# A two-block fp32 network on one core: index scores in tiles of their own, three gates behind the attention's output projection, and input rows scaled on TensorE

## The chip, the core and the metric

The kernel runs as one program on one core of one Trainium2 chip. The metric is the device time of one execution in microseconds (us); the time before is 1074.39 us, the median of three runs. A core has TensorE (PE, matmuls), VectorE (DVE), ScalarE (ACT), GpSimd (POOL) and SyncE (SP, which issues the large transfers).

## What is computed

Two blocks over 256 rows of 1024 channels, in fp32. The first has a conv branch and a sparse-attention branch that share one input projection, gates on both, and a feed-forward part; the second block (two mixers with feed-forward parts) is not touched by the change. Cut to the part that is touched:

```python
stream = concat([meta, x])                      # 16 meta rows + 256 rows, 1024 channels
h = rms_norm(stream, mix_norm_g)
u_conv, q, k, v, q_idx, k_idx, w_idx, gates = split(h @ w_in)
q, k, q_idx, k_idx = rope(...)                  # rotary embedding
a, gate = split(u_conv)                         # conv branch
c = causal_depthwise_conv(a * sigmoid(gate), conv_dw_w, conv_dw_b)      # 31 taps
y_a = silu(layer_norm(c, conv_ln_g, conv_ln_b)) @ conv_pw_out
dots = einsum("qhd,sd->qhs", q_idx, k_idx) * 64 ** -0.5                 # 8 index heads
score = einsum("qh,qhs->qs", w_idx * 8 ** -0.5, relu(dots))
idx = top_k(score with the meta rows always in)                         # a mask for each query
y_b = softmax(q @ k.T over the chosen keys) @ v @ w_o                   # 8 heads of 128
g_a, g_b = split(sigmoid(gates))
stream = stream + (g_a * y_a + g_b * y_b) @ w_merge_out
```

## The kernel before

Channels lie on partitions: the normed input is hT, eight tiles of 128 channels by 272 rows (or 258 rows, the last two meta rows and the 256 others, where only these are wanted). Each fp32 operand of a large product is split into a high part and the rest (whi and wlo of a weight, hT_h and hT_l of an input), and a product is three matmuls, whi with hT_h, whi with hT_l and wlo with hT_h (lines 175 to 177). So a projection to 128 output channels (`proj_tile`) is 24 matmuls into one PSUM buffer of four (ps_acc), and takes one half of a weight chunk. A chunk comes by one transfer on SP (wraw, three buffers); for each half, 128 x 1024, ACT copies the high part (whi, line 134) and DVE subtracts it (wlo, line 136), into six buffers that PE frees by reading them (`emit_split`, `next_half`). Smaller products, transposes and scores go through four other PSUM buffers (ps_wk).

The order of the work on an engine is set when the program is built: a scheduler places the instructions by their dependencies and priorities, parts under a high priority go first, and in the first stretch the order of PE, DVE and ACT is that of the code. At run time each engine takes its instructions in that order, and stands where one waits.

The stretch that the change touches runs from 0 to about 222 us:

- *Start* (lines 282 to 367). A warm-up of WARM = 9 fp32 matmuls of ones (L283); transposes of the 16 meta rows mt (L299); `turn` (L294) transposes the two 128-row tiles of x, eight 128 x 128 blocks each, into px, four PSUM buffers. ACT and DVE sum the squares of the rows (L305, L306, L307, L312), POOL takes the root (L233, a power of -0.5), and `spread` (L290) transposes the roots of all rows, repeated, so that they lie as a row over all partitions (rw). `scaled` (L329, DVE) multiplies px by that row into h, ACT makes hT_h of it with the norm's gain (L333), DVE hT_l (L344). The first two conv projections are interleaved by the list FIRST (L358), the other 14 follow (`proj_tile`).
- *Conv* (lines 365 to 423). 31 taps on 8 tiles: most on DVE (L389), some as products on ACT (L406), which are added by DVE (L412) or, into ysum, by transfers on POOL's queue that add in memory (L410); two rows L423 at the end add ysum.
- *Index scores* (`index_scores`, a generator that its callers advance): for each of two row tiles t and each of 8 heads a matmul (L474) into a ps_wk buffer, a Relu on ACT (L477) into r, one of two buffers of the tag s1, and a weighted sum on DVE (L478).
- *k, v, q projections*, then 16 gate projections in pairs (j = 0 for the conv branch's, j = 1 for the attention's; tanh on ACT into tg, L611), and between them the attention heads in steps: `attend_first` (the two meta rows as queries: L578, L580, L595) is advanced between the first gates, then `attend` of each head i behind gate pair i: scores (L553), softmax (`soft`, L534 and L538 on DVE, L537 and L539 on ACT), transposes (L556, L558), and after every fourth head the product with v (L566, L568).
- *End of the stretch.* The attention's output projection takes oT (8 projections of 24 matmuls; DVE adds the gate, L664). Under high priority the layer norm (LN) of the conv result yc: sums over tiles on DVE (L645, L646), over channels on PE (L648), yc minus the mean (L650), squares on ACT (L652), their sum on DVE (L654), over channels on PE (`rstd_row`, L631, L633 on DVE, the root L635 on POOL, its spread L638 on PE), then yc by the root (L658), Silu (L659) and the split into sT_h and sT_l (L200, L202). The conv's projections read sT (8 of 24 matmuls), and everything behind follows from both. POOL also clears a tile for the second reading of the meta rows (MEMSET mt_again, L677).

Of the kernel before, what the change touches and what calls it, by code (L numbers as in the profile page):

```python
# [59 lines left out]
WARM = 9  # L60
FIRST = []
for _k in range(KT + 1):
    for _j in range(2):
        FIRST += [(_j, 0, 0, _k)] if _k < KT else []
        FIRST += [(_j, 0, 1, _k - 1)] if _k else []
    FIRST += [(0, 1, 0, 3 * (_k - 5) + _i) for _i in range(3) if _k > 4 and 3 * (_k - 5) + _i < KT]
FIRST += [(1, 1, 0, _k) for _k in range(KT)]
PACE = 2
LATER = mybir.DependencyInfo(mybir.DependencyClass.NoSync, mybir.DependencyReason.DATA)
# [15 lines left out]
def tile_hybrid(ctx: ExitStack, tc: tile.TileContext, x, meta, wts, misc, vec, cst, rows, gkw, ng, pos,  # L85
# [36 lines left out]
    def emit_split(upto, later=None):  # L122
        while state["split"] < min(upto, 2 * N_CHUNKS):
# [10 lines left out]
            A.activation(hi, r, AF.Copy)  # L134
# [53 lines left out]
    def proj_tile(ps, xT, a, b, late=False):  # L188
        w = next_half()
        if late:  # L190
# [90 lines left out]
    pj = ps_acc()  # L281
    for _ in range(WARM):
        PE.matmul(pj[:, :P], ones, ones, start=True, stop=True)  # L283
    px = [ps_wk() for _ in range(4)]
    pm = pj[:, :P]
    pr = pj[:, P:P + L]
    rw = mp.tile([P, L], F32, name="rw", tag="sco", bufs=2)
    hm = sc.tile([P, KT, META], F32, name="hm", tag="s3", bufs=3)
    def spread(r, a, n):
        PE.transpose(pr[:, a:a + n], r.to_broadcast([n, P]), ident[:n, :n])  # L290

    def turn(t):
        for k in range(KT):
            PE.transpose(px[k // 2][:, (k % 2) * SEQ + t * P:(k % 2) * SEQ + (t + 1) * P],  # L294
                         xt[t][:, k * P:(k + 1) * P], ident)

    with tc.high_priority(), tc.manual_schedule(engines={ENG.PE, ENG.DVE, ENG.Activation}):
        for k in range(KT):
            PE.transpose(pm[:, k * META:(k + 1) * META], mt[:, k * P:(k + 1) * P], ident[:META, :META])  # L299
        turn(0)  # L300
        sm_ = sc.tile([P, 4], F32, name="sm_", tag="st", bufs=6)
        rm = sc.tile([P, 4], F32, name="rm", tag="st", bufs=6)
        ss = sc.tile([P, 4], F32, name="ss", tag="st", bufs=6)
        rs = sc.tile([P, 4], F32, name="rs", tag="st", bufs=6)
        A.activation(xn[2][:META], mt, AF.Square, accum_out=sm_[:META, 0:1])  # L305
        A.activation(xn[0], xt[0], AF.Square, accum_out=ss[:, 0:1])  # L306
# [9 lines left out]
        for t in range(2):  # L316
            spread(rs[:, t:t + 1], META + t * P, P)
# [18 lines left out]
        for q in range(4):  # L336
            high(2 * q)
            high(2 * q + 1)
            if q == 0:
                emit_split(2, later)  # L340
# [266 lines left out]
    for i in range(KT):  # L607
# [7 lines left out]
        for a in live:  # L615
            next(a)
# [702 lines left out]
```

## Time and profile before

| | |
|---|---|
| three runs | 1075.55, 1074.39, 1074.29 us; median 1074.39 us |
| the profiled execution | 1076.28 us; its span, first to last instruction, 1074.5 us |
| PE busy | 1054.8 us, 98% of the span |
| DVE busy | 739.5 us, 69% |
| ACT busy | 601.0 us, 56% |
| POOL busy | 44.1 us, 4% |
| transfers | 192.37 MB, mean 179 GB/s |

The profiled execution is one of its own and 1.89 us longer than the median; 1.78 us of it lie outside the span. Times of rows are from the start of the span. Matmuls are pipelined, so their durations overlap, and what one costs is the distance from start to start. An engine's idle time is put down to the instruction that released the waiting one. A share of the whole span is a mean over stretches with different limits.

### The profile page before, as it was taken

The page shows a single profiled execution, that of the slowest core. Times are in us where ns is not written, and L with a number is a line of the kernel's source. Part 1 is how long each engine was busy: PE and PEld are TensorE (multiplying, and loading weights), DVE is VectorE, ACT ScalarE, POOL GpSimd, SP SyncE. Part 2 cuts the span into 40 slices and gives each one's busy share as a digit, 9 for nine tenths or more (in the row PEclk, how much of TensorE's full clock was granted, in tenths as well). Part 3 has the DMA queues.
Part 4 walks back from the last instruction along what each step waited for, and adds up shares of the span by engine and source line. Part 5 has one row for each costly group of instructions (what it writes and reads, how often), then busy time and mean ns, then how long its engine had stood idle before and what let it go on. Part 6 is the DMA issues. An engine that isn't in the chain of part 4 may idle for free. (4 is left out here: it accounts for less than half of the span.)

```text
span 1074.5 us, 17515 instructions
## 1 busy us (share of the span) xinstructions
PE 1054.8 (98%) x6989; PEld 954.5 (89%) x6989; DVE 739.5 (69%) x1291; ACT 601.0 (56%) x1051; POOL 44.1 (4%) x52
## 2 busy tenths in 40 slices
PE   8999999999999999999999999999999999999997
PEld 8998998899899999977877999999888878999995
DVE  6899999995776767774577655556674766555555
ACT  6897698564555555567463444446256925444440
POOL 0131002100000000000000000000000000000000
PEclk8999999999999999999999999999999999999999
DMA  8886556564354555454453655557263436555541
GB/s 307 246 201 161 191 166 178 148 220 169 142 197 160 195 182 192 174 185 139 153 202 112 236 196 179 180 191 274 79 215 138 164 131 226 187 195 194 173 144 40
DMA packets 33333, 192.37 MB, mean 179 GB/s; under 512 B 3889, under 2 KB 7857, under 8 KB 12002
## 3 DMA queue, kind: packets, MB, share of 16 engines
q1 hardware_dynamic: 28002, 185.02, 49.7%
q0 software_dynamic: 5248, 6.23, 3.6%
q8 instruction: 55, 0.90, 0.3%
q14 instruction: 28, 0.23, 0.1%
HBM read 183.96 MB, written 1.05 MB: 172 GB/s over the span
## 5 line engine op out<-in xcount | busy, mean ns | idle before, releaser
L136 DVE TENSOR_TENSOR wlo<-wraw,whi 128x1024 fp32r<-128x1024 f32 x320 | 388.5, 1223 | 204.8 <-ACT whi L134 203.9
L134 ACT ACTIVATE whi<-wraw 128x1024 fp32r<-128x1024 f32 x322 | 337.3, 1058 | 302.0 <-PE ps_wk L176 117.7
L176 PE MATMUL ps_wk<-hT_l,whi 128*128 128x256 f32 (+1 forms) x976 | 274.9, 282 | 0.0
L177 PE MATMUL ps_wk<-hT_h,wlo 128*128 128x256 f32 (+1 forms) x976 | 274.6, 281 | 0.0
L175 PE MATMUL ps_wk<-hT_h,whi 128*128 128x256 f32 (+1 forms) x976 | 274.2, 281 | 0.0
L175 PEld LDWEIGHTS ps_wk<-hT_h,whi 128*128 128x128 f32 x976 | 184.4, 189 | 1.1
L176 PEld LDWEIGHTS ps_wk<-hT_l,whi 128*128 128x128 f32 x976 | 184.0, 189 | 1.4
L177 PEld LDWEIGHTS ps_wk<-hT_h,wlo 128*128 128x128 f32 x976 | 184.8, 189 | 0.4
L181 PE MATMUL ps_acc<-whi,rg_h 128*128 128x512 f32 x328 | 131.1, 400 | 0.0
L182 PE MATMUL ps_acc<-wlo,rg_h 128*128 128x512 f32 x328 | 129.6, 395 | 0.0
L183 PE MATMUL ps_acc<-whi,rg_l 128*128 128x512 f32 x328 | 127.1, 395 | 0.0
L175 PE MATMUL ps_acc<-hT_h,whi 128*128 128x258 f32 (+2 forms) x352 | 101.9, 290 | 0.0
L177 PE MATMUL ps_acc<-hT_h,wlo 128*128 128x258 f32 (+2 forms) x352 | 100.7, 286 | 0.0
L176 PE MATMUL ps_acc<-hT_l,whi 128*128 128x258 f32 (+2 forms) x352 | 100.5, 285 | 0.0
L183 PEld LDWEIGHTS ps_acc<-whi,rg_l 128*128 128x128 f32 x328 | 61.6, 188 | 14.7 <-DVE rg_l L202 0.2
L181 PEld LDWEIGHTS ps_acc<-whi,rg_h 128*128 128x128 f32 x328 | 61.6, 188 | 14.1 <-ACT rg_h L200 0.2
L182 PEld LDWEIGHTS ps_acc<-wlo,rg_h 128*128 128x128 f32 x328 | 61.7, 188 | 12.8
L181 PE MATMUL ps_acc<-whi,hT_h 128*128 128x512 f32 (+1 forms) x184 | 71.8, 390 | 0.0
L183 PE MATMUL ps_acc<-whi,hT_l 128*128 128x512 f32 (+1 forms) x184 | 70.8, 385 | 0.0
L182 PE MATMUL ps_acc<-wlo,hT_h 128*128 128x512 f32 (+1 forms) x184 | 70.6, 384 | 0.0
L175 PEld LDWEIGHTS ps_acc<-hT_h,whi 128*128 128x128 f32 x352 | 66.2, 188 | 0.3
L176 PEld LDWEIGHTS ps_acc<-hT_l,whi 128*128 128x128 f32 x352 | 66.3, 188 | 0.2
(950 smaller groups left out, 1561.7 us busy)
## 6 DMA issues: line engine op xcount, KB each, us to landing
wraw<-in_wts_dram SPq DMA_DIRECT2D x166, 1024.0 KB, 5.0
ysum<-zs POOLq DMA_DIRECT2D x10, 258.0 KB, 6.9
x<-in_x_dram SPq DMA_DIRECT2D x4, 512.0 KB, 3.8
lg<-in_rows_dram SPq DMA_DIRECT2D x4, 512.0 KB, 3.6
lb<-in_rows_dram SPq DMA_DIRECT2D x4, 512.0 KB, 5.4
wraw<-in_wts_dram SPq DMA_DIRECT2D x2, 512.0 KB, 6.5
out_dram<-x SPq DMA_DIRECT2D x4, 256.0 KB, 2.0
mraw<-in_misc_dram SPq DMA_DIRECT2D x1, 576.0 KB, 12.3
```

The source lines that it names most:

```text
L134: A.activation(hi, r, AF.Copy)
L136: V.tensor_sub(lo, r, hi.bitcast(F32))
L175: PE.matmul(ps, wh, xh, start=first, stop=False)
L176: PE.matmul(ps, wh, xl, start=False, stop=False)
L177: PE.matmul(ps, wl, xh, start=False, stop=last)
L181: PE.matmul(ps, xh, wh, start=first, stop=False)
L182: PE.matmul(ps, xh, wl, start=False, stop=False)
L183: PE.matmul(ps, xl, wh, start=False, stop=last)
```

## The change

Four edits. (1) *Start:* `turn` is no longer a transpose: it multiplies each block of x by a diagonal matrix of the rows' roots (dg, made by DVE from the identity), as a full fp32 matmul, so that px comes out transposed and scaled; `scaled`, the roots of x in `spread` and their copy rw go. Each row tile's squares are shared, 512 columns on ACT and 512 on DVE, with a root of its own for each. The warm-up is split in 9 and 3 matmuls, the order of the first pair follows the list ARRIVE, DVE casts the second half of the first whi, and the second pair of conv projections takes all products with whi ahead of those with wlo. (2) *Index scores:* the Relus write into r8, one tile for all eight heads of a row tile (it lies where tg will be), and 512 columns at a time: four heads of 128 columns or two of 256 share a PSUM buffer. The generator has one step for each of these groups, and each q projection advances it. (3) *First queries:* `attend_first` is started between the first gates instead of ahead of them, and ends one head later. (4) *Gates:* with LEFT = 3, the gates (j = 0, i = 5, 6, 7) are done behind the attention's eight output projections; the weights are packed in that order.

```diff
-WARM = 9
+WARM = (9, 3)
+ARRIVE = "W0 h0 h1 l0 h2 l1 h3 V0 W1 l2 h4 l3 h5 V1 h6 l4 h7 l5 l6 l7".split()
+LEFT = 3
...
-            A.activation(hi, r, AF.Copy)
+            if h == 0:
+                A.activation(hi[:, :512], r[:, :512], AF.Copy)
+                V.tensor_copy(hi[:, 512:], r[:, 512:])
+            else:
+                A.activation(hi, r, AF.Copy)
...
+        if late == "w":
+            for i, k, j in [(0, k, j) for k in range(KT) for j in range(2)] + [(1, k, 0) for k in range(KT)]:
+                PE.matmul(ps, w[i][:, k * P:(k + 1) * P], xT[j][:, k, a:b],
+                          start=k + i + j == 0, stop=k == KT - 1 and i == 1)
+            return
...
     def turn(t):
         for k in range(KT):
-            PE.transpose(px[k // 2][:, (k % 2) * SEQ + t * P:(k % 2) * SEQ + (t + 1) * P],
-                         xt[t][:, k * P:(k + 1) * P], ident)
+            PE.matmul(px[k // 2][:, (k % 2) * SEQ + t * P:(k % 2) * SEQ + (t + 1) * P],
+                      xt[t][:, k * P:(k + 1) * P], dg[:, t, :], start=True, stop=True)
...
+        def square(t, s_):
+            A.activation(xn[t][:, :512], xt[t][:, :512], AF.Square, accum_out=s_[:, 0:1])
+            V.scalar_tensor_tensor(xn[t][:, 512:], xt[t][:, 512:], 1.0, xt[t][:, 512:], op0=OP.mult, op1=OP.mult,
+                                   accum_out=s_[:, 1:2])
...
+        def diagonal(t, r_):
+            V.tensor_scalar(dg[:, t, :], ident, r_[:, 0:1], math.sqrt(D), op0=OP.mult, op1=OP.mult)
+
+        square(0, s0)
+        root(s0, r0)
+        square(1, s1)
+        diagonal(0, r0)
         turn(0)
...
-            proj_tile(pa[:, :L], hT, 0, L)
-            proj_tile(pg[:, :L], hT, 0, L)
+            proj_tile(pa[:, :L], hT, 0, L, late="w" if i == 1 else False)
+            proj_tile(pg[:, :L], hT, 0, L, late="w" if i == 1 else False)
...
-            for h in range(8):
-                pd = ps_wk()
-                PE.matmul(pd[:, :nk], qi[h // 2][:, t * P:(t + 1) * P], kidx[h % 2][:, :nk],
-                          start=True, stop=True)
-                r = sc.tile([P, SEQ], F32, name="r", tag="s1", bufs=2)[:, :nk]
-                A.activation(r, pd[:, :nk], AF.Relu)
-                V.scalar_tensor_tensor(sco, r, wix[:, t, h:h + 1], vm if h == 0 else sco,
-                                       op0=OP.mult, op1=OP.add)
-                if h == 3:
+            r8 = mp.tile([P, 8, SEQ], F32, name="r8", tag=f"tg{t}")[:, :, :nk]
+            wide = 512 // nk
+            for h0 in range(0, 8, wide):
+                if h0:
                     yield
+                pd = ps_wk().rearrange("p (a b) -> p a b", a=wide)
+                for a in range(wide):
+                    h = h0 + a
+                    PE.matmul(pd[:, a, :], qi[h // 2][:, t * P:(t + 1) * P], kidx[h % 2][:, :nk],
+                              start=True, stop=True)
+                A.activation(r8[:, h0:h0 + wide, :], pd, AF.Relu)
+                for h in range(h0, h0 + wide):
+                    V.scalar_tensor_tensor(sco, r8[:, h, :], wix[:, t, h:h + 1], vm if h == 0 else sco,
+                                           op0=OP.mult, op1=OP.add)
...
         rope(qT[:, h, :], pq[:, :NQ], T0, L, 0)
+        next(scores, None)
...
-    live = [attend_first()]
-    next(live[0])
+    def gate(j, i):
+        pg = ps_acc()
+        proj_tile(pg[:, :NQ], hT, T0, L)
+        A.activation(tg[j][:, i, :], pg[:, :NQ], AF.Tanh, scale=0.5)
+
+    first = attend_first()
+    live = [first]
     for i in range(KT):
         for j in range(2):
-            pg = ps_acc()
-            proj_tile(pg[:, :NQ], hT, T0, L)
-            A.activation(tg[j][:, i, :], pg[:, :NQ], AF.Tanh, scale=0.5)
+            if j or i < KT - LEFT:
+                gate(j, i)
             for a in live:
-                next(a)
+                next(a, None)
         live = [attend(i, t) for t in range(2)]
         for a in live:
             next(a)
+        if i == 0:
+            live.append(first)
...
+    for i in range(KT - LEFT, KT):
+        gate(0, i)
```

The order on PE at the start, in the program before (x_86 and x_87 are the two row tiles, cs holds the identity, rm and rs are the roots of the meta rows and of x):

```order
L283 MATMUL ps_acc<-ones 128x128 x9
L299 MATMUL ps_acc<-cs,mt 128x16 x8
L294 MATMUL ps_wk<-cs,x_86 128x128 x8
L290 MATMUL ps_acc<-cs,rm 128x16
L294 MATMUL ps_wk<-cs,x_87 128x128 x8
L290 MATMUL ps_acc<-cs,rs 128x128 x2
L358 MATMUL ps_acc<-hT_h,whi 128x272 x2
L358 MATMUL ps_acc<-hT_l,whi 128x272
```

The same place in the changed program (L306 is `turn`, L373 the first pair of projections):

```order
L302 MATMUL ps_acc<-ones 128x128 x9
L320 MATMUL ps_acc<-cs,mt 128x16 x8
L321 MATMUL ps_acc<-cs,rm 128x16
L302 MATMUL ps_acc<-ones 128x128 x3
L306 MATMUL ps_wk<-dg,x_86 128x128 x8
L306 MATMUL ps_wk<-dg,x_87 128x128 x5
L373 MATMUL ps_acc<-hT_h,whi 128x272
L306 MATMUL ps_wk<-dg,x_87 128x128
```

The roots of the meta rows and three warm-up matmuls now stand ahead of both turns, and the first products with hT stand among the blocks of the second turn.

The order on DVE at the end of the conv, ahead of the LN's first sum over channels, in the program before (L423 adds ysum, L664 empties an output projection):

```order
L202 TENSOR_TENSOR oT_l<-ps_wk,oT_h 128x4x128
L389 SCALAR_TENSOR_TENSOR yc<-hp,dwh,yc 128x242
L423 TENSOR_TENSOR yc<-yc,ysum 128x1032 x2
L136 TENSOR_TENSOR wlo<-wraw,whi 128x1024
L645 TENSOR_TENSOR sqb<-yc 128x516 x2
L664 SCALAR_TENSOR_TENSOR tg_1520<-tg_1520,ps_acc 128x258
L646 TENSOR_TENSOR sqb<-sqb 128x516
```

The same place in the changed program (L404 is the tap L389, L438 is L423, L143 is L136, L671, L690 and L672 are L645, L664 and L646):

```order
L404 SCALAR_TENSOR_TENSOR yc<-hp,dwh,yc 128x243 x4
L404 SCALAR_TENSOR_TENSOR yc<-hp,dwh,yc 128x242 x2
L438 TENSOR_TENSOR yc<-yc,ysum 128x1032
L143 TENSOR_TENSOR wlo<-wraw,whi 128x1024
L438 TENSOR_TENSOR yc<-yc,ysum 128x1032
L690 SCALAR_TENSOR_TENSOR tg_1487<-tg_1487,ps_acc 128x258
L671 TENSOR_TENSOR sqb<-yc 128x516 x2
L143 TENSOR_TENSOR wlo<-wraw,whi 128x1024
L672 TENSOR_TENSOR sqb<-sqb 128x516
```

The attention's last split oT_l now stands further up, ahead of 13 more taps (before: one), and the first emptying of an output projection stands behind the second sum with ysum. PE's first LN matmul stands behind 120 of the 192 matmuls of the output projection (before: 82), L631 39 matmuls later (before: 73), L638 another 6 later (before: 5), and between it and the first sT matmul stand 27 of them and the 72 of the three gates (before: 32).

The order on POOL's queue around the clearing of mt_again, in the program before:

```order
L410 DMA ysum<-zs_2298 128x2x250
L410 DMA ysum<-zs_2298 128x2x248
L410 DMA ysum<-zs_2299 128x2x244
L410 DMA ysum<-zs_2299 128x2x242
L677 MEMSET mt_again 128x1024
L635 TENSOR_TENSOR rs<-st,mhalf 128x3 x2
```

The same place in the changed program:

```order
L425 DMA ysum<-zs_2173 128x2x250
L425 DMA ysum<-zs_2173 128x2x248
L705 MEMSET mt_again 128x1024
L425 DMA ysum<-zs_2174 128x2x244
L425 DMA ysum<-zs_2174 128x2x242
L661 TENSOR_TENSOR rs<-st,mhalf 128x3 x2
```

The clearing, which waits for the last readers of the tile's memory (the attention's products with v), now stands ahead of the last two sums into ysum.

## Rows read from the trace of the kernel before

**Rows 1.** The page, part 1: busy time, share of the span, instructions.

```profile
PE 1054.8 (98%) x6989; PEld 954.5 (89%) x6989; DVE 739.5 (69%) x1291; ACT 601.0 (56%) x1051; POOL 44.1 (4%) x52
```

**Rows 2.** Stretches: PE, PEld, DVE, ACT, POOL busy (count), clock, DMA share, GB/s.

```profile
20.00:90.00 70.00, 68.24 (x547) 67.62 (x545) 65.37 (x116) 61.48 (x120) 12.59 (x12) 1.00 0.87 241
90.00:203.00 113.00, 111.84 (x847) 103.18 (x846) 111.46 (x289) 87.50 (x220) 16.07 (x17) 1.00 0.59 161
```

**Rows 3.** DVE's waits, 20 to 203: us in total, times, longest.

```profile
DVE wlo L136 <- ACT whi L134: 2.9, 5, 1.5
DVE yc L412 <- ACT z L406: 0.8, 1, 0.8
DVE yc L423 <- DMA ysum<-zs: 0.7, 1, 0.7
DVE hp L365 <- ACT th L364: 0.4, 1, 0.4
DVE t L431 <- ACT sw L430: 0.4, 1, 0.4
DVE oT_l L202 <- ACT oT_h L200: 0.3, 1, 0.3
```

**Rows 4.** PE's timeline at the start: start, us, instructions, [idle before, releaser].

```profile
1.15 4.21 PE L283 MATMUL ps_acc<-ones 128*128 128x128 f32 x18 [1.15 <-DVE ones L221]
...
8.36 1.65 PE L294 MATMUL ps_wk<-cs,x 128*128 128x128 f32 x8
...
12.96 0.99 PE L358 MATMUL ps_acc<-hT_h,whi 128*128 128x272 f32 x2 [2.73 <-ACT hT_h L333]
```

**Rows 5.** Stretches as in rows 2; the clock is the third number from the end.

```profile
13.00:14.00 1.00, 1.00 (x3) 0.75 (x3) 0.96 (x3) 1.00 (x2) 0.00 (x0) 0.50 1.06 430
...
19.00:20.00 1.00, 1.00 (x7) 1.00 (x7) 1.00 (x4) 1.00 (x2) 0.00 (x0) 0.61 0.00 0
```

**Rows 6.** DVE's timeline at the end of the start.

```profile
19.15 0.87 DVE L344 SCALAR_TENSOR_TENSOR hT_l<-h,vecs,hT_h 128x256 fp32r<-128x256 f32 x2
19.95 4.62 DVE L136 TENSOR_TENSOR wlo<-wraw,whi 128x1024 fp32r<-128x1024 f32 x4
24.48 0.43 DVE L365 SCALAR_TENSOR_TENSOR hp<-th,ps_acc 128x272 f32<-128x272 f32 x1
```

**Rows 7.** PE's waits, 80 to 95.

```profile
PE ps_wk L474 <- ACT r L477: 1.8, 2, 1.6
```

**Rows 8.** ACT's waits, 80 to 95.

```profile
ACT r L477 <- DVE sco L478: 3.5, 3, 1.8
```

**Rows 9.** PE's timeline, first queries and the end of the stretch.

```profile
130.02 0.26 PE L580 MATMUL ps_wk<-kT,q 128*8 128x16 f32 x4 [0.79 <-DVE q L578]
...
194.00 1.02 PE L568 MATMUL ps_wk<-pTz,vt 128*128 128x512 f32 x2
...
203.17 1.14 PE L648 MATMUL ps_wk<-sqb,ones 128*128 128x258 f32 x4 [0.40 <-DVE sqb L646]
...
204.39 0.28 PE L175 MATMUL ps_acc<-oT_h,whi 128*128 128x258 f32 x1
...
212.86 0.62 PE L631 MATMUL ps_wk<-ones,sqb 128*128 128x1 f32 x6
...
215.68 0.58 PE L638 MATMUL ps_wk<-cs,rs 128*128 128x128 f32 x3 [1.39 <-POOL rs L635]
...
221.59 0.39 PE L176 MATMUL ps_acc<-sT_l,whi 128*128 128x258 f32 x1 [0.47 <-DVE sT_l L202]
```

**Rows 10.** DVE's timeline, last row of the LN's first sum.

```profile
202.43 0.69 DVE L646 TENSOR_TENSOR sqb<-sqb 128x516 f32<-128x516 f32 x1
```

**Rows 11.** POOL's timeline, 180 to 218.

```profile
194.87 1.44 POOL L677 MEMSET mt_again<- 128x1024 f32 x1
213.82 1.80 POOL L635 TENSOR_TENSOR rs<-st,mhalf 128x3 f32<-128x3 f32 x1 [17.51 <-DVE st L633]
```

**Rows 12.** Transfers issued from 190 to 200: count, KB, us to landing.

```profile
ysum<-zs POOLq DMA_DIRECT2D x1, 242.0 KB, 4.3
```

More of the change, by code (lines that the diff above doesn't have):

```diff
@@ L59 @@
 WIX = 1
-WARM = 9
+WARM = (9, 3)
+ARRIVE = "W0 h0 h1 l0 h2 l1 h3 V0 W1 l2 h4 l3 h5 V1 h6 l4 h7 l5 l6 l7".split()
 FIRST = []
-for _k in range(KT + 1):
+for _n, _z in enumerate(ARRIVE):
     for _j in range(2):
[L64 to L67, printed above, removed]
+        for _k in range(KT):
+            for _a, _b in ((0, 0), (0, 1), (1, 0)):
+                _w, _h = "WV"[_a] + str(_j), "hl"[_b] + str(_k)
+                if _z in (_w, _h) and {_w, _h} <= set(ARRIVE[:_n + 1]):
+                    FIRST.append((_j, _a, _b, _k))
 PACE = 2
+LEFT = 3
 LATER = mybir.DependencyInfo(mybir.DependencyClass.NoSync, mybir.DependencyReason.DATA)
@@ L279, in tile_hybrid @@
     nc.sync.dma_start(mraw, misc.rearrange("p (a b) -> p a b", a=KT))
-    pj = ps_acc()
-    for _ in range(WARM):
-        PE.matmul(pj[:, :P], ones, ones, start=True, stop=True)
+    pj, pz = ps_acc(), ps_acc()
     px = [ps_wk() for _ in range(4)]
     pm = pj[:, :P]
-    pr = pj[:, P:P + L]
-    rw = mp.tile([P, L], F32, name="rw", tag="sco", bufs=2)
     hm = sc.tile([P, KT, META], F32, name="hm", tag="s3", bufs=3)
-    def spread(r, a, n):
-        PE.transpose(pr[:, a:a + n], r.to_broadcast([n, P]), ident[:n, :n])
+    dg = mp.tile([P, 2, P], F32, name="dg", tag="sco", bufs=2)
@@ L292, in turn, with warm @@
+    rw = sc.tile([P, META], F32, name="rw", tag="s4", bufs=3)
+    def warm(n):
+        for _ in range(n):
+            PE.matmul(pz[:, :P], ones, ones, start=True, stop=True)
     def turn(t):
         for k in range(KT):
-            PE.transpose(px[k // 2][:, (k % 2) * SEQ + t * P:(k % 2) * SEQ + (t + 1) * P],
-                         xt[t][:, k * P:(k + 1) * P], ident)
+            PE.matmul(px[k // 2][:, (k % 2) * SEQ + t * P:(k % 2) * SEQ + (t + 1) * P],
+                      xt[t][:, k * P:(k + 1) * P], dg[:, t, :], start=True, stop=True)
@@ L297, in tile_hybrid @@
     with tc.high_priority(), tc.manual_schedule(engines={ENG.PE, ENG.DVE, ENG.Activation}):
+        warm(WARM[0])
+        sm_ = sc.tile([P, 4], F32, name="sm_", tag="st", bufs=6)
+        rm = sc.tile([P, 4], F32, name="rm", tag="st", bufs=6)
+        s0 = sc.tile([P, 4], F32, name="ss", tag="st", bufs=6)
+        s1 = sc.tile([P, 4], F32, name="ss", tag="st", bufs=6)
+        r0 = sc.tile([P, 4], F32, name="rs", tag="st", bufs=6)
+        r1 = sc.tile([P, 4], F32, name="rs", tag="st", bufs=6)
@@ L314, in tile_hybrid @@
[L314 to L318 removed]
+        PE.transpose(pj[:, P:P + META], rm[:META, 0:1].to_broadcast([META, P]), ident[:META, :META])
+        V.tensor_copy(rw, pj[:, P:P + META])
+        V.tensor_mul(hm, pm.rearrange("p (k t) -> p k t", k=KT), rw[:, None, :].to_broadcast([P, KT, META]))
@@ L1238, in _pack @@
     pair = lambda z: z.reshape(2, 8, P, HALF).transpose(1, 0, 2, 3).reshape(16, P, HALF)
+    g = pair(g)
+    left = [2 * i for i in range(KT - LEFT, KT)]
+    keep = [i for i in range(2 * KT) if i not in left]
     gl = a["gla_w_in_2"][0]
```

60 lines of the change are left out of this document (22 added, 38 removed).

## The prediction

> **What bounds the kernel now.** I read the page's busy shares first: TensorE (PE) is busy 98% of the span [rows 1], so a change of order can win only what PE idles, and the clock that it runs at. Next the busy time by stretch: from 20 to 90 us VectorE (DVE) is busy 65.37 of 70 us and from 90 to 203 us 111.46 of 113 [rows 2], although it has only 69% over the whole span. So up to the layer norm of the conv branch (LN, whose first matmul is L648 at 203.17) two engines are full side by side, and the end of that stretch is set by whichever is later. In before they meet almost exactly: PE waits 0.40 us at L648 for DVE's L646, not at all at L631, 1.39 us at L638 and 0.47 us at the first sT matmul, 221.59 [rows 9]. All that the change touches lies ahead of that sT matmul, and behind it both programs run the same work; so I take **the start of sT** as the milestone, and its shift as the change of the time. The profiled run took 1076.28 us (span 1074.5 and 1.78 around it), 1.89 above the median 1074.39; a shift carries over to the median unchanged.
>
> **The change part by part, on PE's side.** (a) *Start.* Before, PE idles 2.73 us up to 12.96 [rows 4]; behind that gap its granted clock is 0.50 (1.2 GHz of 2.4) for some 6.8 us: the stretch 13 to 14 has 0.50, that from 19 to 20 has 0.61 [rows 5]. By the count of its matmuls the first pair of conv projections is done at about 22.35. After, both row tiles go through 16 full fp32 matmuls against a diagonal instead of 16 transposes. The nearest row for their price is the warm-up L283, nine of the same shape in 4.21 us, 0.468 each, where eight transposes take 1.65, 0.206 each [rows 4]; so 16 x 0.468 = 7.5 us against 3.3, and half of the 7.5 if the clock is up. The first diagonal: DVE now does the meta rows first (behind the transposes of mt), then its half of the squares, POOL's root and the diagonal itself; replayed with the durations of before's rows of these kinds I estimate 9.1. So PE works from 9.2 without the gap: eight matmuls to 12.9, the first h tile at 13.4, and the conv matmuls behind it warm if the clock rises by about 13. DVE's low tiles then pace it, and the last ends near 19.65 where the last L344 ended at 19.15 + 0.8 = 19.95 [rows 6]: the four scalings L329 are gone, one cast and the diagonals added. I take the first pair done at 20.0: 2.35 us for PE, 0.3 for DVE. Ends for PE: +4 (clock up at once) and -1 (low through both turns).
>
> The Trainium skill, "TensorE: Matmul & The Clock Gate", Terms, says that a transpose mode makes an fp32 transpose four times as fast. The rows above show 0.468 against 0.206, a ratio of 2.3, and they decide the sum; what the other ratio would do is rival 4.
>
> (b) *Index scores.* PE waits 1.8 us for L477 [rows 7], because L477 itself waits 3.5 us for a DVE row that still reads its two-deep buffer [rows 8]. With all eight heads in a tile of their own, ACT waits for PE alone: 1.8 us of PE. (c) *First queries.* PE waits 0.79 at L580 [rows 9]; twelve more matmuls stand ahead of it, 1.4 us of cover: 0.79 gone. (d) *Three gates later.* 72 matmuls move from the last three heads to just ahead of sT: PE's work is unchanged, but they cover the 0.47 at sT. With L648's 0.40 [rows 9], PE alone would gain 2.35 + 1.8 + 0.79 + 0.47 + 0.40 = 5.8 us.
>
> **On DVE's side.** This is where I choose, for that gain counts only as far as DVE's chain to the LN comes earlier too. Up to L646 DVE does two low-half splits fewer (52 instead of 54 by the order), 2 x 1.13 = 2.27 us (four take 4.62 and the next row starts 4.53 after them [rows 6]). The start gives 0.3. Its idle time can shrink: between 20 and 203 us it waits 4.8 us for ACT, 2.9 of it for whi, and 0.7 for a ysum transfer [rows 3]. ACT is late there because it stands behind L477 and behind buffers that PE frees; both come earlier. I take the 4.8 us on ACT as gone and leave the 0.7. So L646 ends 0.3 + 2.27 + 4.8 = 7.4 us earlier.
>
> Behind L646 the cover is thinner. A projection matmul takes 0.119 there (71 of them from 204.39 to 212.86 [rows 9]). Before, 73 stand between L648 and L631, after 39: 34 x 0.119 = 4.0 us less. DVE's own work there, from L646's end at 203.12 [rows 10] to L631 at 212.86, 9.74 us, loses one split (1.13) and becomes 8.6; PE's becomes 0.8 for L648 + 39 x 0.119 = 5.45. So PE would stand 3.1 us at L631, for L654. Then 2.82 us from L631 to L638 as before (POOL's root L635 takes 1.80, unhidden [rows 9, 11]), 0.5 for L638, and 27 + 72 matmuls, 11.8 us, until sT. From L646 to sT: 8.6 + 2.82 + 0.5 + 11.8 = 23.7 us, against 221.59 - 203.12 = 18.5 before: **5.2 us longer**, since the gates that filled earlier time now stand in this stretch.
>
> Sum, with DVE's chain setting the pace: 7.4 - 5.2 = **2.2 us earlier**. PE alone would allow 5.8, so DVE's chain is the later one and gives the time: 1074.39 - 2.2 = 1072.2 (the profiled run 1074.1). PE then has over 3 us in hand when it comes to L648 and waits there for L646, or just ahead for a ps_acc buffer that DVE's L664 empties behind L423; that is the same wait.
>
> POOL's queue is moved too: MEMSET mt_again, which waits for the attention's last readers, now stands ahead of the last two ysum transfers. The last L568 ends near 195.0 [rows 9], the MEMSET takes 1.44 [rows 11], the transfers one more microsecond to issue and 4.3 to land [rows 12]: DVE's second L423 can start some 7 to 8 us after the last L568. The attention ends 12 to 13 us earlier (8.5 of gates, and the lead), near 182.5; 190 is within 0.5 us of when DVE gets there. I cost it at nothing; if the attention gains less than that, it costs up to 1.5.
>
> **The rivals.** (1) *DVE isn't the later one; PE sets the pace.* For it: PE's 98%, and conv taps can fill DVE's waits. Against it: DVE is busy 111.46 of 113 us [rows 2]. Then all of the 5.8 us: 1068.6. Chance 0.2. (2) *ACT stays late:* DVE's 4.8 us of waits stay, and the 34 matmuls missing between L648 and L631 decide: 0.3 + 2.27 - 5.2 = -2.6, so 1077.0. It is slower from the point where less than 2.6 of the 4.8 us vanish. For it: ACT is busy 61.48 of 70 us from 20 to 90 [rows 2], and a Relu of 512 columns holds its queue longer than one of 128. Against it: its own 3.5 us at L477 go [rows 8]. Chance 0.14, a third of it within the bound. (3) *The start doesn't do what it says:* the clock stays at 1.2 GHz through both turns and the first projections, DVE is 1 us later instead of 0.3 earlier, and the 0.9 us of its waits that hang on the first gates' th and whi stay: 2.2 - 1.3 - 0.9 = 0, so 1074.4. For it: PE's 4.21 us of fp32 ahead of the transposes [rows 4] left nothing that shows a faster rate in them. Chance 0.18. (4) *A matmul against a diagonal costs more than L283:* at four times a transpose's 0.206, 0.82, the 16 take 13.2 us, 5.7 more than by L283; both engines stand behind it: 2.2 - 5.7 = -3.5, so 1077.9. The skill's ratio (the Terms named above) would give this. Against it: L283 has their shape and type. Chance 0.03.
>
> **How the numbers follow.** About 0.2% (2.1 us) is what a measurement of this kernel can tell from no change, so the line for faster is 1072.24, and the forecast lies on it. Forecast as it stands (1071.0 to 1073.5) 0.45: faster 0.25, same 0.20. Rival 1: faster 0.20. Rival 2: slower 0.09, same 0.05. Rival 3: same 0.14, faster 0.02, slower 0.02. Rival 4: slower 0.03. Together faster 0.47, same 0.39, slower 0.14. The range runs from rival 1's 1068.6 to 1076.0: above that are left the worse part of rival 2 and rival 4, below it a start worth 4 us with PE setting the pace; together under 2 in 10.
>
> **What would show it.** Right: the granted clock at 1.00 by about 13 us and no PE gap of 2 us behind 9.2; no wait of L474 for ACT or of L477 for DVE; DVE's waits for whi between 20 and 90 us under 1 us; L648 near 195.5, waiting for L646; a wait of about 3 us at L631 for L654, and none at sT. Wrong: L648 as late as 199 with DVE's waits on ACT still there (rival 2); no wait at L631 and L648 near 193 (rival 1); 0.50 in the clock to 19 us (rival 3); a wait of L423 for ysum over 1 us, which would be POOL's MEMSET.

## The result: 13.6 us slower

The changed kernel takes 1088.59 us (median of four runs, 1087.33 to 1089.70) where the kernel before took 1074.97 beside it (four runs, 1074.29 to 1075.95): a ratio of 1.0122 [1.0108, 1.0137]. The forecast was 1072.2, with a range up to 1076.0; the time lies 12.6 us above the end of the range. The profiled execution took 1088.34, its span 1086.5 us, 12.0 longer than before's 1074.5.

The page, part 1, of the kernel after (as [rows 1]): TensorE (PE) is busy 5.9 us longer, the work of VectorE (DVE) is the same to 0.8.

```profile
PE 1060.7 (98%) x7009; PEld 961.2 (88%) x7009; DVE 738.7 (68%) x1293; ACT 597.8 (55%) x1039; POOL 45.0 (4%) x53
```

Stretches of the kernel after; the columns are those of [rows 2], with the granted clock third from the end:

```profile
9.00:10.00 1.00, 1.00 (x6) 1.00 (x6) 0.59 (x3) 0.84 (x2) 0.38 (x1) 0.50 1.06 442
12.00:13.00 1.00, 1.00 (x12) 1.00 (x10) 0.00 (x0) 0.37 (x1) 0.00 (x0) 1.00 1.05 413
20.00:90.00 70.00, 68.05 (x549) 67.70 (x549) 62.73 (x110) 60.30 (x118) 12.64 (x12) 1.00 0.85 232
90.00:203.00 113.00, 106.20 (x780) 97.58 (x779) 108.96 (x290) 82.17 (x204) 16.06 (x17) 0.97 0.56 152
131.00:138.00 7.00, 5.05 (x26) 5.00 (x27) 7.00 (x18) 2.81 (x5) 0.00 (x0) 0.51 0.68 217
202.00:207.00 5.00, 5.00 (x29) 4.92 (x28) 4.16 (x6) 0.64 (x1) 0.00 (x0) 0.66 0.47 149
207.00:213.00 6.00, 3.72 (x30) 3.52 (x29) 5.53 (x16) 4.25 (x10) 0.00 (x0) 1.00 0.21 90
213.00:223.00 10.00, 9.40 (x45) 8.70 (x44) 5.92 (x15) 2.74 (x3) 1.79 (x1) 0.50 0.31 107
```

From 90 to 203 us PE is busy 106.20 us where it was busy 111.84, and in three stretches its granted clock is down to or near 0.50, 1.2 GHz instead of 2.4: before, the clock is 1.00 in all of them. The count of matmuls bears the clock out: from 213 to 223 only 45 records start in 9.40 busy us. The lows are not spread evenly; each stands behind a wait in PE's timeline of the kernel after (columns as in [rows 4]):

```profile
8.68 4.58 PE L306 MATMUL ps_wk<-dg,x 128*128 128x128 f32 x26 [1.99 <-DVE dg L336]
...
132.95 0.28 PE L600 MATMUL ps_wk<-kT,q 128*8 128x16 f32 x4 [4.29 <-DVE q L598]
...
201.79 0.39 PE L182 MATMUL ps_acc<-oT_h,whi 128*128 128x258 f32 x1 [2.45 <-DVE tg L690]
206.30 1.03 PE L674 MATMUL ps_wk<-sqb,ones 128*128 128x258 f32 x4
212.48 0.36 PE L182 MATMUL ps_acc<-oT_h,whi 128*128 128x258 f32 x1 [2.28 <-DVE tg L690]
215.37 0.96 PE L657 MATMUL ps_wk<-ones,sqb 128*128 128x1 f32 x6
218.53 0.88 PE L664 MATMUL ps_wk<-cs,rs 128*128 128x128 f32 x3 [0.60 <-POOL rs L661]
233.00 0.28 PE L182 MATMUL ps_acc<-sT_h,whi 128*128 128x258 f32 x1
233.12 0.28 PE L183 MATMUL ps_acc<-sT_l,whi 128*128 128x258 f32 x1
```

These are the rows that answer to [rows 9] (L600 is L580, L674 is L648, L657 is L631, L664 is L638). The wait at the first queries has grown from 0.79 to 4.29 us. The two waits for tg are new: PE's output projection needs a PSUM buffer (ps_acc) that DVE empties in L690, and L690 stands in DVE's order behind the second sum with ysum. The milestone, the first matmul with sT, moves from 220.12 to 233.00, 12.9 us later, and 853.5 us follow it where 854.4 did: all of the loss lies ahead of it, as the prediction took it. The row at 221.59 [rows 9], which the prediction takes for it, is the eighth matmul with sT in before, behind the wait of 0.47 us. The first is this one:

```profile
220.12 0.28 PE L175 MATMUL ps_acc<-sT_h,whi 128*128 128x258 f32 x1
```

DVE's waits in the same stretch as [rows 3], in the kernel after:

```profile
DVE wlo L143 <- ACT whi L141: 6.3, 4, 4.7
DVE yc L438 <- DMA ysum<-zs: 1.1, 1, 1.1
DVE t L446 <- ACT sw L445: 1.0, 2, 0.8
DVE yc L427 <- ACT z L421: 0.8, 1, 0.8
```

The prediction let DVE's waits on ScalarE (ACT) go; the largest of them grew from 2.9 to 6.3 us. Three timelines of the kernel after show where. DVE at 53 us, and its last row ahead of the LN's first sum (as [rows 10]):

```profile
53.80 1.22 DVE L143 TENSOR_TENSOR wlo<-wraw,whi 128x1024 fp32r<-128x1024 f32 x1 [4.66 <-ACT whi L141]
...
204.00 0.69 DVE L672 TENSOR_TENSOR sqb<-sqb 128x516 f32<-128x516 f32 x1
```

ACT at the same place:

```profile
51.91 0.91 ACT L421 ACTIVATE zs<-hp,dwh 128x258 f32<-128x258 f32 x2 [4.65 <-DMA ysum<-zs]
52.73 1.04 ACT L141 ACTIVATE whi<-wraw 128x1024 fp32r<-128x1024 f32 x1
```

And POOL, which issues the in-memory sums:

```profile
52.42 0.87 POOL L425 DMA_DIRECT2D ysum<-zs  x1 [7.23 <-DMA ysum<-zs]
...
189.13 0.95 POOL L705 MEMSET mt_again<- 128x1024 f32 x1 [0.61 <-PE ps_wk L588]
```

Read from the bottom: the sums run one behind another (POOL waits 7.23 us for the one before), ACT's next product L421 has no free slot until one has landed, the weight split whi stands behind that product in ACT's order, and DVE's wlo waits for whi. The same two waits are there in before, shorter (ACT's, then DVE's):

```profile
51.13 0.51 ACT L406 ACTIVATE zs<-hp,dwh 128x258 f32<-128x258 f32 x1 [1.69 <-DMA ysum<-zs]
52.62 1.22 DVE L136 TENSOR_TENSOR wlo<-wraw,whi 128x1024 fp32r<-128x1024 f32 x1 [1.53 <-ACT whi L134]
```

ACT comes to this place about 2 us earlier in the changed kernel and goes on 0.8 us later, so its lead ends as a longer wait for the sum. MEMSET, the prediction's worry on this queue, ran at 189.13, ahead of need.

### The profile page after: what moved, and what is told of

Same layout as the page of the kernel before. It is cut to its first block, busy times and chain, and to the rows that moved or that the text cites. A ratio compares the mean times of both kernels' runs of the same rounds, so it can differ in the third digit from the quotient of the medians.

```text
span 1086.5 us, 17532 instructions
## 1 busy us (share of the span) xinstructions
PE 1060.7 (98%) x7009; PEld 961.2 (88%) x7009; DVE 738.7 (68%) x1293; ACT 597.8 (55%) x1039; POOL 45.0 (4%) x53
## 5 line engine op out<-in xcount | busy, mean ns | idle before, releaser
L143 DVE TENSOR_TENSOR wlo<-wraw,whi 128x1024 fp32r<-128x1024 f32 x320 | 388.1, 1222 | 212.7 <-ACT whi L141 211.9
L182 PE MATMUL ps_acc<-hT_h,whi 128*128 128x258 f32 (+2 forms) x336 | 98.7, 294 | 0.0
L183 PE MATMUL ps_acc<-hT_l,whi 128*128 128x258 f32 (+2 forms) x336 | 96.9, 288 | 0.0
L184 PE MATMUL ps_acc<-hT_h,wlo 128*128 128x258 f32 (+2 forms) x336 | 96.7, 288 | 0.0
L190 PEld LDWEIGHTS ps_acc<-whi,rg_l 128*128 128x128 f32 x328 | 61.6, 188 | 14.7 <-DVE rg_l L214 0.2
L184 PEld LDWEIGHTS ps_acc<-hT_h,wlo 128*128 128x128 f32 x336 | 64.4, 192 | 0.1
```

Source lines behind the costliest of these rows:

```text
L143: V.tensor_sub(lo, r, hi.bitcast(F32))
L182: PE.matmul(ps, wh, xh, start=first, stop=False)
L183: PE.matmul(ps, wh, xl, start=False, stop=False)
L184: PE.matmul(ps, wl, xh, start=False, stop=last)
L190: PE.matmul(ps, xl, wh, start=False, stop=last)
```

## The experiments

All ratios are against the kernel before on the same chip. "L646" is the start of DVE's last row ahead of the LN's first sum under whatever line number it has, "sT" the start of the first matmul with sT, "low" the sum of (1 - clock) over 195 to 235 us, in us. The last three columns are of the profiled execution, the ratio is of all executions.

| kernel | ratio [95%] | L646 | sT | low |
|---|---|---|---|---|
| before | 1 | 202.43 | 220.12 | 0 |
| after | 1.0122 [1.0108, 1.0137] | 204.00 | 233.00 | 6.8 |
| s_start | 1.0013 [1.0001, 1.0025] | 204.43 | 220.77 | 0 |
| s_index | 1.0022 [1.0011, 1.0034] | 203.18 | 222.40 | 1.7 |
| s_first | 0.9995 [0.9982, 1.0008] | 201.10 | 218.80 | 0 |
| s_left | 1.0117 [1.0090, 1.0144] | 202.19 | 235.00 | 6.8 |
| u_left | 1.0003 [0.9991, 1.0015] | 204.90 | 221.14 | 0 |
| left_1 | 1.0044 [1.0028, 1.0060] | 202.83 | 225.65 | 1.7 |
| left_early | 1.0061 [1.0042, 1.0080] | 204.16 | 225.75 | 5.1 |
| left_fill | 1.0095 [1.0077, 1.0113] | 200.89 | 230.61 | 0 |
| after_early | 1.0014 [1.0003, 1.0026] | 205.33 | 221.57 | 0 |
| before_taps | 1.0003 [0.9991, 1.0015] | 197.64 | 219.90 | 0 |
| uleft_taps | 1.0021 [1.0009, 1.0033] | 200.19 | 222.67 | 0 |
| before_nodma | 0.9968 [0.9955, 0.9982] | 200.57 | 216.94 | 0 |
| s_start_nodma | 1.0021 [1.0011, 1.0030] | 201.79 | 221.79 | 1.7 |
| before_dveadd | 1.0068 [1.0044, 1.0093] | 206.00 | 229.79 | 6.8 |
| s_start_dveadd | 1.0079 [1.0054, 1.0104] | 205.95 | 231.24 | 10.2 |
| u_left_dveadd | 1.0087 [1.0060, 1.0114] | 207.69 | 232.21 | 8.5 |

The differences in sT are the differences of the medians to about 1.7 us, but for s_left, whose profiled execution was the longest of its four (1090.43 us; 2.7 us apart). L646 says much less: between before and after it moved 1.6 us, sT 12.9.

### Each edit alone

*The start alone* (s_start): the diff's hunks on `turn`, `square`, `root`, `diagonal`, the warm-up and the order of the first two pairs.

> The kernel before with the edit of the start alone (diagonals, shared squares, order of the first two pairs). Two theories for the 13 us that the whole change loses. Cover: the loss is made where the three gates were taken out from under the attention and the norm of the conv result; then this edit alone gains what it gains at the start, 2 to 3 us (1072). Lead: any edit that brings TensorE ahead loses it again where TensorE next waits for VectorE, and a wait of over 2 us costs the clock too; then this edit alone gives 1074 to 1078, with a wait of over 2 us and a granted clock of 0.50 behind it somewhere between 80 and 215 us.

*The index scores alone* (s_index): eight heads in a tile of their own.

```diff
-                r = sc.tile([P, SEQ], F32, name="r", tag="s1", bufs=2)[:, :nk]
...
+            r8 = mp.tile([P, 8, SEQ], F32, name="r8", tag=f"tg{t}")[:, :, :nk]
```

> The kernel before with the index scores in tiles of their own alone. Both theories: 1073 to 1075; the 1.8 us wait of L474 for the Relu goes. Cover says a gain of about 1.5 us; lead says no change, the 1.8 us come back as waits for VectorE at the first queries or the norm.

*The first queries alone* (s_first):

```diff
-    next(live[0])
...
+        if i == 0:
+            live.append(first)
```

> The kernel before with the first queries started behind twelve more matmuls and ended one head later, alone. Cover: 0.8 us of wait at L580 gone, 1073.6 to 1074.4. Lead: no change, within 1 us of before. If this edit itself moves VectorE's copy of the first queries further back, the wait at L580 is over 2 us with the clock at 0.50 behind it, and the time is 1077 or more.

*The three late gates alone* (s_left):

```diff
+LEFT = 3
...
+            if j or i < KT - LEFT:
+                gate(j, i)
...
+    for i in range(KT - LEFT, KT):
+        gate(0, i)
```

> The kernel before with the three gates moved behind the attention's output projection, alone. Cover: this edit carries the loss: waits of 2 us or more ahead of L648 and before L631, the granted clock at 0.50 in part of 195 to 225 us, 1081 to 1086. Lead: TensorE has no extra lead here, so the waits are under 2 us each, the clock holds, and the time is 1074 to 1077.

Measured: 1077.75, 1078.39, 1075.37 and 1088.61 us beside 1076.38. The late gates alone cost 12.2 us, nearly all of the loss and more than the 10 that were expected at most. The start and the index scores alone are 1.4 and 2.0 us slower than before, with intervals that exclude no change; for the index scores both theories had expected a gain or none. PE's waits from 20 to 235 us with the late gates alone:

```profile
PE ps_acc L176 <- DVE tg L670: 8.3, 2, 5.5
PE ps_wk L475 <- ACT r L478: 3.2, 2, 1.6
```

and with the index edit alone:

```profile
PE ps_wk L585 <- DVE q L583: 3.5, 1, 3.5
PE ps_wk L643 <- POOL rs L640: 1.4, 1, 1.4
```

and with the start alone:

```profile
PE ps_wk L488 <- ACT r L491: 4.4, 2, 2.4
PE ps_wk L594 <- DVE q L592: 0.6, 1, 0.6
```

What an early edit wins is lost at the next place where DVE or ACT is behind: the start's lead at the index scores (1.8 us of waits become 4.4, with the clock at 1.2 GHz behind them), the index's gain at the first queries (0.79 becomes 3.5). The first queries' edit can't be told from no change (0.9995), and PE's wait there is 0.6 us still.

### The change without the late gates

u_left is the changed kernel with one number changed:

```diff
-LEFT = 3
+LEFT = 0
```

> The whole change without the gates' edit (LEFT = 0): start, index scores and first queries. If the gates' edit carries the loss, this is within 2 us of before (1074 to 1078); by the sum of the three single edits (+0.1%, +0.2%, -0.05%) it is 1079. If the edits need each other to lose, it is over 1081.

1076.93 beside 1076.69: no difference. So the three other edits don't add up to their 4.9 us together either, and the late gates carry the loss in company as they do alone. left_1, s_left with LEFT = 1, asks whether the cost goes with their number:

> The gates' edit alone with one gate moved instead of three. If the loss grows with the missing cover gate by gate: a third of it, 1080. If the clock makes it a step: with 2.85 us less ahead of the norm the first wait is about 2.5 us and the loss is either under 2 us (clock holds, 1076 to 1078) or 4 us and more (clock falls, 1080 to 1082).

1081.45 beside 1076.69: one gate costs 4.8 us, three cost 12.2 (1088.61 - 1076.38), some 4 us for each.

### Is it the gates' place, and is it the clock?

left_early is s_left with the gates ahead of the output projection, where they give PE work while DVE finishes the conv:

```diff
+    for i in range(KT - LEFT, KT):
+        gate(0, i)
     conv()
...
-    for i in range(KT - LEFT, KT):
-        gate(0, i)
```

> The gates' edit alone, but the three gates stand right behind the attention and ahead of the output projection (weights packed so), where ScalarE empties their buffers, not VectorE. If the loss comes from what stands ahead of the norm (an output projection's buffers wait for VectorE, gates' buffers don't), there is no wait over 1 us between 185 and 222 and the time is 1075 to 1078, as before. If it comes from taking the gates out from under the heads, the loss of 12 us stays, 1086 or more.

left_fill is s_left with 72 more matmuls, 72 x 0.119 = 8.6 us of TensorE's work, in the output projection: the products of one of its eight tiles run three times and of the next twice.

```diff
+        proj_tile(py[:, :NQ], oT, 0, NQ, again={3: 3, 4: 2}.get(m, 1))
```

> The gates' edit alone (s_left), with 72 matmuls added that change no result: the fourth output projection is computed three times over and the fifth twice, 8.5 us of TensorE work in the place where s_left waits 5.47 and 2.80 us for VectorE. Theory 1, the waits cost twice, once themselves and once as a clock of 1.2 GHz behind them (about 7 us of the 12): with TensorE busy the clock stays at 1.00 from 195 to 225 and the time falls to 1080 to 1083, although there is more work. Theory 2, VectorE's chain alone sets the time and the clock behind the waits costs nothing: 1088 to 1090. Theory 3, TensorE sets the time: 8.5 us more, 1097.

left_early takes 1082.58 us and left_fill 1086.02, against 1088.61 for s_left. left_early wins back half of the loss, where its theories had all of it or nothing: 5.9 us are left, with a new wait of PE at the LN itself and 5.1 us of low clock:

```profile
PE ps_wk L656 <- DVE sqb L654: 3.9, 1, 3.9
```

left_fill is the telling one for the clock. By the medians it is 2.6 us faster than s_left, but the two intervals overlap, and it lies between the two forecasts nearest to it (1080 to 1083, 1088 to 1090). What its time shows is that 8.6 us more to do cost nothing. In the profiled executions sT starts 4.4 us earlier (230.61 against 235.00), with L646 1.3 us earlier. Its stretches, and the clock in them:

```profile
195.00:205.00 10.00, 7.41 (x59) 7.10 (x59) 7.85 (x14) 1.48 (x5) 0.00 (x0) 1.00 0.33 77
...
215.00:225.00 10.00, 10.00 (x86) 10.00 (x85) 10.00 (x22) 8.18 (x17) 0.00 (x0) 1.00 0.41 148
```

The same of s_left:

```profile
195.00:205.00 10.00, 4.53 (x26) 4.04 (x24) 6.36 (x8) 1.06 (x1) 0.00 (x0) 0.83 0.35 79
...
215.00:225.00 10.00, 8.72 (x58) 8.28 (x58) 6.13 (x15) 5.47 (x10) 1.79 (x1) 0.82 0.32 107
```

With the waits of 5.5 and 2.8 us at ps_acc filled, the clock stays at 2.4 GHz, although a wait of 2.59 us at the LN is left, and 86 matmuls start from 215 to 225 instead of 58. So s_left pays twice: for standing still, and for running at half speed behind it. The Trainium skill, "TensorE: Matmul & The Clock Gate", "A second HAM failure mode: psum-queue depth-cycling", describes this pattern in a bf16 kernel, where TensorE runs short between groups of matmuls as PSUM buffers come round and loses throughput by it. These runs agree, with 6.8 us of low clock without the filling and none with it.

after_early is the same repair in the whole change, whose gates' loop and weights are moved as in left_early:

```diff
-    parts = [..., g[keep], _ws(a["attn_w_o"][0]), g[left], ...]
+    parts = [..., g[keep], g[left], _ws(a["attn_w_o"][0]), ...]
```

> The whole change, with the three late gates written ahead of the output projection instead of behind it. Theory A (the place of the gates costs: TensorE runs dry ahead of or behind them, once for the wait and once more at 1.2 GHz): the loss falls from 13 us to between 3 and 7, as it did with the gate edit alone (14 us against 6), with no wait of 2 us at the gates' own first weight load and the clock's loss between 195 and 225 us below 5.5. Theory B (it is the number of gates that come late, wherever they stand): the loss stays within 2 us of 13.

1078.26 beside 1076.07, a ratio of 1.0014: 2.2 us of loss where the whole change loses 13.6. That is a smaller loss than was expected of the place (3 to 7). Its waits on PE from 20 to 230 us:

```profile
PE ps_wk L600 <- DVE q L598: 3.4, 1, 3.4
PE ps_wk L495 <- DVE qi L448: 2.2, 1, 2.2
PE ps_wk L676 <- DVE sqb L674: 0.9, 1, 0.9
```

and two of its stretches:

```profile
195.00:205.00 10.00, 10.00 (x86) 9.97 (x84) 9.07 (x18) 5.20 (x7) 2.35 (x2) 1.00 0.70 159
...
215.00:225.00 10.00, 10.00 (x81) 9.58 (x81) 9.78 (x24) 9.36 (x19) 0.88 (x1) 1.00 0.54 199
```

L646 starts 1.3 us later than in the changed kernel (205.33 against 204.00), and yet sT starts 11.4 us earlier: from one to the other it takes 16.2 us instead of 29.0. Where the 72 matmuls stand decides the loss; that DVE's chain ends late is common to both.

### Does DVE or the queue of sums set the pace?

Leaving 16 of DVE's taps out, about 7 us of its work (before_taps, and uleft_taps in the change without late gates):

```diff
+                    if n in (3, 4, 5, 6):
+                        continue
```

> The kernel before without the VectorE taps 3 to 6 of the 31 (16 instructions, some 7 us of VectorE, so the conv is not the reference's). Theory 1, up to the norm VectorE's chain and TensorE's are equally long in before: less VectorE work frees little, only what TensorE waits at L648, L638 and sT, and the time falls by 0.5 to 2.5 us. Theory 2, VectorE alone sets the end of the stretch: the time falls by 5 to 7 us.

> Start, index scores and first queries as in the change, gates as before (u_left), and the same taps left out. Theory 1 (what TensorE gains by these edits, 2.3 + 1.8 + 0.8 us, is lost because VectorE is not earlier): with VectorE 7 us lighter the gain appears, 3 to 5 us below before_taps, and the wait at L600 falls from 4.3 to under 2 us. Theory 2 (the edits' own waits, at the first queries above all, eat the gain): the wait at L600 stays and the time is within 1.5 us of before_taps.

1076.98 and 1079.19 beside 1076.24: nothing won, where at least 0.5 us had been expected of the first. L646 comes 4.8 us earlier in before_taps (197.64) and sT 0.2 (219.90), since PE now waits 3.7 us at the index scores, with 1.7 us of low clock there. Less work on DVE in the conv doesn't help: what runs beside it moves in the order too.

Leaving four of the 24 in-memory sums out (before_nodma, and s_start_nodma with the start's edit):

```diff
-                elif far:
+                elif far and not (i0 == 0 and q in (1, 3)):
```

> The kernel before with the same four in-memory sums left out (the conv is not the reference's). VectorE waits 1.53 us there in before, so at most that much moves: within 1.5 us of before by the queue's theory, under 0.5 us if VectorE's work is the limit.

> The start's edit alone (s_start), with four of the in-memory sums of the conv's first half left out: their products are made by ScalarE but not added, so the conv is not the reference's. In s_start VectorE stands 3.84 us near 53 behind ScalarE, which waits for a product's buffer that a transfer on POOL's queue has not yet read. If this queue is where the start's lead is lost, that wait falls under 1 us, L646 ends 2 to 3 us earlier than in s_start and the time is 2 to 3 us below s_start and 1 to 2 below before_nodma. If VectorE's work is the limit anyway, the time moves by under 1 us.

1073.27 and 1078.71 beside 1076.24. Without these sums before is 3 us faster, twice what was expected at most: the waits of DVE and ACT for them are real. But with the start's edit on top the time goes up by 5.4 instead of down by 2.3: L646 is only 1.2 us later than in before_nodma and sT 4.9 (three waits of 0.9 to 2.1 us at the LN, 1.7 us of low clock). So a free queue doesn't let the start's lead through.

Doing these four sums on DVE instead (before_dveadd; s_start_dveadd and u_left_dveadd with the start alone and with the change without late gates):

```diff
-                far = q % 2 == 1
+                far = q % 2 == 1 and not (i0 == 0 and q in (1, 3))
```

> Before, with the two far products of each lane pair in the conv's first half added by VectorE instead of by in-memory sums of the transfer queue: four tensor_add more on VectorE, four sums fewer on the queue, the same result. Theory A (ScalarE's products wait for room in the slots that the sums free, and VectorE's splits wait for ScalarE): between 3 lower and 1 lower than before, as with the sums left out altogether (3.0 to 3.4 lower), less what four more additions cost; no index wait over 0.5 us. Theory B (VectorE is full there and each of its instructions counts): 1 to 4 us longer.

> The edit of the start alone, with the same four sums moved to VectorE. Theory A (the start's 2.3 us are lost at the index scores because ScalarE waits for the sums): 1 to 2.5 us below the kernel before with the sums moved. Theory B (the lead is lost to whichever engine is next, so it returns nothing): within 1 us of it, or above, with waits of over 1 us on TensorE and 1.2 GHz behind them.

> The change without the late gates, with the same four sums moved to VectorE. Theory A: 2 to 5 us below before (start 2.3, index 1.8 and first queries 0.8 of which the wait of 4.3 us on VectorE's copy of q takes some back). Theory B: within 2 us of before, with the wait on the copy of q still over 3 us and the clock at 1.2 GHz behind it, since VectorE is full from 90 to 130 us.

1084.11, 1085.65 and 1086.52 beside 1076.07: 8 us longer and more, where the theory of the sums' queue expected a gain and the other at most 4 us of loss. Four additions of 0.69 us, 2.8 together, put L646 3.6 us later in before_dveadd (what makes up the rest wasn't followed), and sT starts 9.7 us later (229.79 against 220.12), with the waits and the clock of the late gates, in a kernel that has none of them. Its waits from 20 to 230 us:

```profile
PE ps_acc L175 <- DVE tg L664: 6.6, 2, 3.8
PE ps_wk L638 <- POOL rs L635: 1.3, 1, 1.3
```

and the stretch behind the first of them:

```profile
205.00:210.00 5.00, 3.87 (x14) 3.49 (x15) 3.49 (x7) 0.21 (x1) 0.00 (x0) 0.50 0.63 217
```

So in before DVE's end of the conv has next to nothing in hand: PE reaches the same buffer at about the same time. That a late L646 alone isn't the cause shows in u_left and s_start, where it starts 2.5 and 2.0 us later than in before and no wait at ps_acc opens. What goes with these waits is how far PE is ahead of DVE: the time from PE's first matmul with oT to the first row in which DVE empties an output projection (L664), 14.7 us in before:

```profile
187.37 0.48 PE L175 MATMUL ps_acc<-oT_h,whi 128*128 128x258 f32 x1
...
202.09 0.42 DVE L664 SCALAR_TENSOR_TENSOR tg<-tg,ps_acc 128x258 f32<-128x258 f32 x1
```

In the ten kernels without a wait of PE for tg it is 9.7 to 16.8 us (u_left 14.0, after_early 9.7). In the seven with one it is 17.0 to 21.9 and the first wait grows with it: 2.14 us at 17.0 (s_start_nodma), 2.45 at 19.0 (after), 3.78 at 20.3 (before_dveadd), 5.47 at 21.9 (s_left). left_fill also has 21.9, with its 8.6 us of filling inside. DVE late and PE early come to the same, and the low clock adds as much as the waits or more (6.6 us of waits and 6.8 of low clock in before_dveadd, 4.7 and 6.8 in after). The start's edit on top of the moved sums is 1.5 us slower by the medians and the three edits together 2.4, both within the noise.

No version here that computes all of it can be told to beat the kernel before; the nearest is s_first, 0.9995.

## Why the prediction was wrong

**Bounds: right. Milestone: right in kind, read from the wrong row.** Two full engines meet at the LN, all of the loss lies ahead of sT, and behind it 0.9 us came back (853.5 against 854.4 us). But the 18.5 us from L646 to sT in before run to the eighth matmul with sT; to the first they are 220.12 - 203.12 = 17.0. The forecast of 23.7 counts to the first, so the stretch was to grow by 6.7 us and not by 5.2, and the prediction's own sum for sT is 0.7 us earlier, not 2.2. By itself this slip doesn't leave the range.

**(a) Start: right in itself.** The first h tile came at 13.16 (13.4 predicted), the pair was done at about 20.6 by the count of matmuls (20.0), before at 22.35; the clock was 1.00 from 12 us on (13). DVE's first hp row started 3.3 us earlier, 2.3 of it two splits that now stand behind it. PE waited 1.99 us for the first diagonal and went on at 8.68 (9.2 predicted), with the clock at 0.50 from 9 to 11 us. A matmul against the diagonal cost less than L283's 0.468: two records stand for one (13 matmuls are x26), so from 9 to 10 us three start in a microsecond at clock 0.50, and from 12 to 13 six at 1.00, about 0.33 and 0.17 us each. Rivals 3 and 4 are out. But alone this edit gives +1.4 us, not -2.3: the 5.8 us of PE's side add up the gains place by place, and PE's lead is lost at the next wait.

**(b) and (c) Index scores, first queries: the waits go, others come.** PE no longer waits for L477's successor, and ACT's wait for DVE is gone. In its place PE waits 2.0 us at the index scores for DVE's qi, and 4.29 at the first queries for DVE's q, with 3.4 us of low clock behind (the stretch 131 to 138). Here the step that failed is "0.79 gone": 1.4 us of matmuls were put in as cover, against a wait that a lead of PE's lengthens by as much as the lead is. DVE is busy 111.46 of 113 us there [rows 2], the very number that said so.

**(d) DVE's chain: the term that failed first, "I take the 4.8 us on ACT as gone".** L646 was to end 7.4 us earlier and ends 1.6 later (204.00 + 0.69 against 203.12), 9.0 us of the miss. It isn't DVE's work: from 20 us to the end of L646 it fell by 3.6 us, where 2.6 were forecast. Its idle time from 20 to 203 was to fall by 4.8 and rose by 5.1 (from 6.17 to 11.31). Taking the waits on ACT as gone rested on ACT being held by L477; it was held by the slots of the in-memory sums, for which ACT waits 4.65 us at 52 us. [Rows 3] show only the last link (wlo behind whi), not ACT's releaser. By itself a late L646 costs little or nothing, as after_early and u_left show; it counts here because these 7.4 us were to pay for the 72 matmuls behind the meeting.

**(d) From L646 to sT: the mechanism was right, its size not.** 23.7 us were forecast, 17.0 are there in before, and it took 28.3 (233.00 - 204.69), 4.6 more than forecast: 10.7 to L657 (8.6 forecast), 3.2 to L664 (2.8) and 14.5 from there (12.3). So the 12.9 us by which sT is late are 6.7 of thinner cover, as the prediction's own method has it, 1.6 of DVE's chain and these 4.6. The thinner cover is there, but the place of the wait was wrong: PE doesn't stand at L631 for L654 (L657 starts without a wait), it stands 2.45 us ahead of the LN and 2.28 behind it, at ps_acc for L690. The prediction named this wait for the first of them and called it the same wait; what it left out is the clock. From 202 to 223 us the clock takes 5 x 0.34 + 10 x 0.50 = 6.7 us, more than the size missed here. Where it is low PE is the late one: DVE's last L680 ends at 214.14, and PE comes to L657 at 215.37. The sum priced every wait at its own length, although [rows 4] and [rows 5] show the clock at 0.50 for 6.8 us behind a gap of 2.73.

**Rivals.** Rival 2 is the nearest: DVE's waits on ACT stay and the missing matmuls decide. It was put at 1077.0, since the waits were only to stay, not to grow, and the clock was not in its price. Rival 1 fell with s_left, where PE has the same work and the time is 12.2 us longer. POOL's MEMSET cost at most the 1.1 us wait of L438 for ysum, 0.4 more than in [rows 3], and POOL's two rows behind it wait for the sum before them (1.49 us) and for ACT's product (3.74), not for it.

**What stays open.** Why the low clock follows one wait and not another of the same length. A wait of 1.39 us at L638 leaves the clock at 1.00 in before, and the same 1.39 us in s_index is followed by 1.7 us of low clock. A wait of 2.59 us at the LN in left_fill is followed by none, 3.4 us at L600 in after_early by none and 4.3 in u_left by 3.4. And of the 2.2 us that after_early still loses, the waits at L495 and L600 are the likely cause, which wasn't tried apart.

## What to carry to other kernels

Where two engines are both full and meet at one place, look for what fills the one when the other is late: moving independent matmuls from ahead of that meeting to behind it cost 12.2 us here although no work was added. Moving them ahead of the output projection gave 6.3 of these back, and in the whole change 11.4 of 13.6. Price a wait of TensorE with the stretch at half clock that may follow, and a lead that an edit gives it with the next wait on the engine that is full. When a wait on an engine is taken as gone, follow that engine's own releaser first.

## What the runs showed of the hardware

TensorE's granted clock fell to 0.50 behind waits as short as 1.39 us (s_index at 217 us), while the same wait in before, up to 215.68, left it at 1.00. So more work need not cost time: 8.6 us of extra matmuls in s_left's waits took its low clock from 6.8 us to none, and left_fill was not slower (1086.02 against 1088.61).

The record of the clock can be wrong by itself. The profile of after_early gives 1.00 from 10 to 13 us, where 16 matmul records start:

```profile
10.00:13.00 3.00, 3.00 (x16) 3.00 (x15) 0.83 (x3) 0.41 (x1) 0.00 (x0) 1.00 1.01 415
```

In the kernel after 12 start in the single microsecond from 12 to 13 at 1.00, and 6 from 9 to 10 at 0.50; so after_early runs at 1.2 GHz there and its record doesn't say so. The Trainium skill, "TensorE: Matmul & The Clock Gate", "Seeing it yourself", warns that these records have been seen to be unreliable, and this row agrees. For the other lows told of here the count of matmuls agrees with the record.

An in-memory sum of 242 to 258 KB landed 3.3 to 8.2 us after its issue in the kernel after (24 of them, median 6.5). POOL stood up to 7.23 us for the one before, and ScalarE 4.65 us for the slot that one of them read.
